# c_gate and h_b of six channel groups computed by tokens, 1024 columns at once, with two seven-product pairs of k-tiles, and a transpose by TensorE

## The chip, the cores and the metric

One core of a Trainium2 chip runs the kernel. The metric is device time of one execution in microseconds (us). Engines: TensorE (PE), VectorE (DVE), ScalarE (ACT), GpSimd (POOL), SyncE (SP, which only issues transfers here).

## The reference

An encoder layer over 256 tokens of 2048 channels, in float32. What touches the change is the second branch, a gated short convolution along the tokens:

```
proj = rmsnorm(h, norm_w) @ w_in          # 9 x 2048 columns
q, v, f_fwd, f_bwd, z_a, b_gate, c_gate, h_b, z_b = split(proj)
o_a = head_rmsnorm(hgrn2(silu(q), v, f_fwd, f_bwd)) * silu(z_a)
y_b = b_gate * short_conv(c_gate * h_b, conv_w)     # width 3, centred, per channel
o_b = rmsnorm(y_b, conv_norm_w) * silu(z_b)
h = h + concat([o_a, o_b]) @ w_out
```

A gate with a second input and a last norm follow.

## The kernel before

**Precision.** A float32 product is made of three products of a rounded high part (`hi`) and the rest (`lo`): hi x hi, hi x lo, lo x hi. The input x, scaled by `norm_w`, is kept split as `xs` (16 k-tiles of 128 channels, hi and lo, 256 tokens). The norm factor per token, `rx`, is multiplied in afterwards.

**Weights.** `Stream` (lines 28 to 134) brings the weights in the order of use. SP loads a `raw` tile of 1 MB (three buffers, and the early ones of the output stage a fourth); each is split into parts of 1024 columns, `spl` (five buffers): ACT casts the high part (line 121), DVE subtracts it for the low part (line 122). `get` asks for three parts ahead of the one in use, at high priority.

**Two ways to multiply.** `gemm_in` (432) gives channels on partitions: a weight k-tile stands still, `xs` streams past, 512 columns (hi and lo of x) and then 256, 32 such pairs for one product of 256 channels. It takes two of the four PSUM banks of the pool `psg`; `evac` (482) empties each with an ACT copy into `r` and a DVE add. `gemm_vz` (456) with `half` (551) gives tokens on partitions: x stands still and 512 weight columns stream. It computes two blocks of 512 columns together, so it takes all four `psg` banks (two token halves by two blocks). Of the eight pairs of k-tiles (q = 0 to 7), those listed in `VZ_SUMS` are multiplied with seven products of 2x2 blocks in place of eight (sums of x made in advance by `act_sums` and `act_split`; sums of weights made in the `raw` tile by three DVE adds, `add_up`, line 79; four more banks for extra products). Such a pair has four `spl` parts instead of two.

**The stage that changes** (924 to 984) is a loop over eight groups of 256 channels. Each group makes four products with `gemm_in`, c_gate (CG), h_b (HB), b_gate (BG), z_b (ZB), then: POOL normalises CG and multiplies by HB into `ub` (channels by tokens, with a zero column at either end); DVE does the convolution into `cg`; POOL multiplies by BG; the square is summed into `ysum`; POOL normalises ZB (`by_norms`), ACT takes its sigmoid `szb`, DVE and POOL multiply all into `cg`; ACT and DVE split `cg` into `mixb` hi and lo. In groups 1 to 4 sums of `mixa` are made too (`sa`, `sb`, `suma`), and in groups 2 to 4 sums of `mixb`, both for the output product.

**Transfers beside.** In this stage the sums of w_out for the later output product are prepared in DRAM: `prepare` copies two blocks into `sums` (SP queue, line 330), `add_up` (332) adds on POOL's queue in three steps. `pump`, called after POOL's operations, does one step at a time, six a group; 16 such sums, 48 steps.

**Order.** A scheduler places the instructions of each engine by priority in the program; each engine runs its own in that fixed order.

## Time and profile before

| | |
|---|---|
| median of 3 runs | 1113.97 us (1111.71 to 1114.72) |
| the profiled execution | 1112.2 us, of which 1110.5 are its span |
| mean granted clock of PE | 0.998 |
| transfers over the span | 260.44 MB, mean 235 GB/s |
| groups 2 to 7 of the stage | some 568 to 835 us |

A row of the timeline has start, length, engine, line, operation, output and inputs, and in brackets the idle time before it and what ended it. SPq is an issue of a transfer by SP. PE's matmuls overlap, so their pitch is read from their starts, not their lengths. In the views of transfers a queue has packets, MB and its share of 16 engines' time.

### The profile page before, as it was taken

What the parts mean: (1) busy time and instruction counts of PE and PEld (TensorE: products, weight loads), DVE (VectorE), ACT (ScalarE), POOL (GpSimd) and SP (SyncE); (2) the same over time, 40 slices, a digit from 0 to 9 for tenths busy, and PEclk for the clock granted to TensorE, in tenths of its full rate; (3) what the DMA queues carried; (4) which work ended last, traced back from release to release, by engine and by line L of the source; (5) the groups of instructions that cost most, each with busy time, mean ns of one, the idle gap of its engine ahead of it and who ended that gap; (6) DMA issues with size and microseconds to landing.
All of it is one profiled execution on the core that took longest, in us unless ns stands there. A gap on an engine that the chain in (4) does not pass through costs nothing.

```text
span 1110.5 us, 16882 instructions
## 1 busy us (share of the span) xinstructions
PE 1100.5 (99%) x6455; PEld 945.7 (85%) x6455; DVE 851.4 (77%) x1127; ACT 677.3 (61%) x946; POOL 269.1 (24%) x215
## 2 busy tenths in 40 slices
PE   9999999999999999999999999999999999999997
PEld 8888888888888888888888888888888888888886
DVE  7799578896889778997657758856667888887673
ACT  6786577667876697575545535535546575575562
POOL 1045015203530325043334223424331000000101
PEclk9999999999999999999999999999999999999999
DMA  9755454564457744758999998999979887887542
GB/s 340 272 187 190 153 190 157 171 242 153 161 162 258 292 152 152 231 172 228 298 310 250 270 334 231 282 345 254 288 196 306 318 299 286 286 312 253 193 133 76
DMA packets 69808, 260.44 MB, mean 235 GB/s; under 512 B 7008, under 2 KB 16608, under 8 KB 52192
## 3 DMA queue, kind: packets, MB, share of 16 engines
q1 hardware_dynamic: 60480, 242.25, 62.1%
q0 software_dynamic: 8960, 16.78, 10.0%
q8 instruction: 51, 0.84, 0.3%
q10 hardware_dynamic: 288, 0.34, 0.1%
q14 instruction: 29, 0.24, 0.1%
HBM read 257.25 MB, written 35.65 MB: 264 GB/s over the span
## 4 chain that ended last, share of the span: by engine, by line
PE 98%; DMA 1%; ACT 0%; SPq 0%; DVE 0%; DVEq 0%; issue 0%; ACTq 0%
PE a L427 37%; PE a L425 19%; PE avz L547 3%; PE avz L548 3%; PE avz L549 3%; PE pg L1027 3%; PE pg L1026 3%; PE pg L1028 3%; PE pa L547 2%; PE pa L548 2%; PE pa L549 2%; PE a L446 1%; PE a L448 1%; PE a L447 1%; PE pb_sc L548 1%; PE pb_sc L549 1%
## 5 line engine op out<-in xcount | busy, mean ns | idle before, releaser
L122 DVE TENSOR_TENSOR spl<-raw,spl 128x1024 fp32r<-128x1024 f32 (+2 forms) x419 | 505.0, 1219 | 163.6 <-ACT spl L121 160.2
L427 PE MATMUL a<-xs,spl 128*128 128x512 f32 x1792 | 617.3, 395 | 0.6 <-ACT spl L121 0.6
L121 ACT CAST spl<-raw 128x1024 fp32r<-128x1024 f32 (+2 forms) x419 | 414.1, 999 | 255.0 <-PE a L425 81.9
L425 PE MATMUL a<-xs,spl 128*128 128x256 f32 x1792 | 483.8, 278 | 0.0
L427 PEld LDWEIGHTS a<-xs,spl 128*128 128x128 f32 x1792 | 332.2, 188 | 73.6 <-ACT spl L121 1.0
L425 PEld LDWEIGHTS a<-xs,spl 128*128 128x128 f32 x1792 | 334.6, 188 | 5.8 <-DVE spl L122 0.5
L1143 POOL TENSOR_TENSOR hh<-hh,fw 128x512 f32<-128x512 f32 (+1 forms) x9 | 11.0, 1227 | 250.7 <-ACT gt L1142 248.0
L487 ACT COPY r<-a 128x256 f32<-128x256 f32 x112 | 40.5, 368 | 37.3 <-PE a L425 35.8
L547 PE MATMUL avz<-spl,xs 128*128 128x512 f32 x138 | 54.0, 391 | 0.0
L549 PE MATMUL avz<-spl,xs 128*128 128x512 f32 x138 | 53.7, 389 | 0.0
L548 PE MATMUL avz<-spl,xs 128*128 128x512 f32 x138 | 53.7, 389 | 0.0
L1026 PE MATMUL pg<-spl,ht 128*128 128x512 f32 (+1 forms) x120 | 45.2, 377 | 0.0
L1027 PE MATMUL pg<-spl,ht 128*128 128x512 f32 (+1 forms) x120 | 45.1, 376 | 0.0
L1028 PE MATMUL pg<-spl,ht 128*128 128x512 f32 (+1 forms) x120 | 45.0, 375 | 0.0
L716 POOL TENSOR_TENSOR qc<-pf,ge 128x256 f32<-128x256 f32 x16 | 18.3, 1148 | 105.8 <-ACT dd L706 91.8
L492 POOL TENSOR_TENSOR xf<-xf,rbc 128x1024 f32<-128x1024 f32 x8 | 19.9, 2486 | 94.0 <-DVE rbc L403 50.2
L121 ACT CAST spl<-early 128x1024 fp32r<-128x1024 f32 (+1 forms) x29 | 28.7, 990 | 19.1 <-PE pb_y L549 7.5
L122 DVE TENSOR_TENSOR spl<-early,spl 128x1024 fp32r<-128x1024 f32 (+1 forms) x29 | 32.9, 1147 | 9.2 <-ACT spl L121 8.8
L547 PE MATMUL pa<-spl,mixa 128*128 128x512 f32 x88 | 34.5, 392 | 0.0
L549 PE MATMUL pa<-spl,mixa 128*128 128x512 f32 x88 | 34.3, 389 | 0.0
L548 PE MATMUL pa<-spl,mixa 128*128 128x512 f32 x88 | 34.2, 389 | 0.0
L716 POOL TENSOR_TENSOR kc<-dd,ge 128x256 f32<-128x256 f32 x16 | 27.7, 1728 | 19.8 <-DVE dd L707 13.6
(321 smaller groups left out, 1641.7 us busy)
## 6 DMA issues: line engine op xcount, KB each, us to landing
raw<-in_w_in_dram SPq DMA_DIRECT2D x106, 1024.0 KB, 6.9
raw<-in_w_in_dram SPq DMA_DIRECT2D x100, 256.0 KB, 3.9
raw<-in_w_out_dram SPq DMA_DIRECT2D x36, 512.0 KB, 5.2
sums<-in_w_out_dram SPq DMA_DIRECT2D x32, 512.0 KB, 10.6
raw<-in_w_in_dram SPq DMA_DIRECT2D x26, 512.0 KB, 5.2
raw<-sums SPq DMA_DIRECT2D x13, 1024.0 KB, 5.3
raw<-in_w_gate_dram SPq DMA_DIRECT2D x9, 1024.0 KB, 5.1
sums<-in_w_out_dram POOLq DMA_DIRECT2D x16, 512.0 KB, 10.1
```

The source lines that it names most:

```text
L121: self.nc.scalar.copy(out=v[:, :, 0], in_=r)
L122: self.nc.vector.tensor_tensor(out=v[:, :, 1], in0=r, in1=v[:, :, 0], op=ALU.subtract)
L425: pe.matmul(a[:, :T], lhsT=lhsT, rhs=xs[:, kt, 0, :], start=False, stop=(kt == NKT - 1))
L427: pe.matmul(a, lhsT=lhsT, rhs=xs[:, kt, :, :].rearrange("p s n -> p (s n)"), start=(kt == 0), stop=False)
L487: act.copy(out=r, in_=acc[m][:, 1, :])
L547: pe.matmul(acc, lhsT=ah, rhs=w[:, 0], start=start, stop=False)
L548: pe.matmul(acc, lhsT=ah, rhs=w[:, 1], start=False, stop=False)
L549: pe.matmul(acc, lhsT=al, rhs=w[:, 0], start=False, stop=stop)
L716: pool.tensor_tensor(out=c64(dst[:, d]), in0=c64(src[:, d, :, half * P : (half + 1) * P]), in1=g.unsqueeze(3).broadcast_to([P, 2, 2, CH]), ...
L1026: pe.matmul(acc[m], lhsT=lh, rhs=wh, start=(kt == 0), stop=False)
L1027: pe.matmul(acc[m], lhsT=lh, rhs=wl, start=False, stop=False)
L1028: pe.matmul(acc[m], lhsT=ll, rhs=wh, start=False, stop=(kt == nk - 1))
```

## The change

For groups 2 to 7, c_gate and h_b of two groups (512 channels each) are one product by tokens, `gemm_pair`, the general form of `gemm_vz`, with pairs q = 2 and 4 as seven products. Three such products (groups 2, 4, 6) replace twelve `gemm_in`. DVE combines the extra products, adds the main ones, and multiplies c_gate, h_b and `rx2` (the square of `rx`); PE turns the result to channels by tokens in eight transposes per product, 12 k-tiles into the next BG, and ACT copies it to `ub`. The convolution then follows. The weights of these products come in four transfers of 256 KB (rows of 2 KB) for each `raw` tile; 1 MB in one transfer (rows of 8 KB) before. The x sums for q = 2 and 4 are kept in the last quarter of `mixa`, the scaled output of the last two heads waits in SBUF and not PSUM, and `mixb` is eight tiles. In groups 2 to 7 `pump` is called four times a group and four times in each of the new products.

```diff
+    CH_SUMS = (2, 4)
+    for i in range(2):
         for c in (B_CG, B_HB, B_BG, B_ZB):
             blocks[c, i] = sum((ws.add(w_in[c + i, h]) for h in range(2)), [])
+    for i in range(2, 8, 2):
+        blocks[B_CG, i] = []
+        for q in VZ_ORDER:
+            srcs = [
+                [w_in[c + i + b, q // 4, :, 2 * (q % 4) : 2 * (q % 4) + 2] for b in range(2)] for c in (B_CG, B_HB)
+            ]
+            blocks[B_CG, i].append(ws.add_own(*srcs) if q in CH_SUMS else ws.add(*srcs[0], *srcs[1]))
+        for ii in (i, i + 1):
+            for c in (B_BG, B_ZB):
+                blocks[c, ii] = sum((ws.add(w_in[c + ii, h]) for h in range(2)), [])
...
+        dve.tensor_tensor(out=rx2, in0=rx, in1=rx, op=ALU.mult)
...
-    def gemm_vz(i, vt, zt):
+    def gemm_pair(name, sums_of, ids, get):
-        acc = [psg.tile([P, 512], F32, tag="g", name=f"avz{i}_{b}") for b in range(4)]
+        acc = [psg.tile([P, 512], F32, tag="g", name=f"a{name}_{b}") for b in range(4)]
...
-        for q1, q5, q6, q7 in half(main, extra, VZ_ORDER, VZ_SUMS, blocks[B_V, i], xs, xq[0], True):
+        for q1, q5, q6, q7 in half(main, extra, VZ_ORDER, sums_of, ids, xs, xq, True):
+            vt, zt, d = get()
...
+    def convolved(i, ut):
+        for ii in (i, i + 1):
+            tp = psm.tile([P, 2, T], F32, tag="xy"[ii % 2], name=f"ut{ii}")
+            for h in range(2):
+                c = (2 * (ii % 2) + h) * P
+                for m in range(2):
+                    pe.transpose(tp[:, h, m * P : (m + 1) * P], ut[:, m, c : c + P], ident)
+            act.copy(out=ub[ii % 2][:, :, 1 : T + 1], in_=tp)
+    def gemm_ch(i):
+        def get():
+            a, b = (bp.tile([P, 2, 512], F32, tag=f"late{e}", name=f"ch{i}_{e}") for e in range(2))
+            return a, b, early[:, 0:512]
+        for z in range(4):
+            at(5 + 10 * z, pump)
+        a, b = gemm_pair(f"ch{i}", CH_SUMS, blocks[B_CG, i], get)
+        with tc.high_priority(offset=300):
+            for m in range(2):
+                dve.scalar_tensor_tensor(
+                    out=a[:, m], in0=a[:, m], scalar=rx2[:, m : m + 1], in1=b[:, m], op0=ALU.mult, op1=ALU.mult
+                )
+        at(12, lambda: convolved(i, a))
     for i in range(8):
-        cg = ctmp.tile([P, 2, T], F32, tag="cg", name=f"cg{i}", bufs=2)
-        evac(gemm_in(B_CG, i, TURNED if i % 2 == 0 else {}), lambda m: cg[:, m, :], ctmp)
-        hb = ctmp.tile([P, 2, T], F32, tag="hb", name=f"hb{i}", bufs=2)
-        evac(gemm_in(B_HB, i, {} if i else TURNED), lambda m: hb[:, m, :], ctmp)
         u = ub[i % 2]
-        by_norms(cg, rbc2, 2)
-        pump()
-        pool.tensor_tensor(out=u[:, :, 1 : T + 1], in0=cg, in1=hb, op=ALU.mult)
-        pump()
+        if i < 2:
...
+        elif i % 2 == 0:
+            gemm_ch(i)
+        kick = {} if i % 2 else TURNED
+        hb = ctmp.tile([P, 2, T], F32, tag="hb", name=f"bg{i}", bufs=2)
+        evac(gemm_in(B_BG, i, kick), lambda m: hb[:, m, :], ctmp)
```

How the order moves is shown at three places. The first is PE's queue in the changed kernel where ZB of group 1 (`a_1_1`, its second bank) ends and the first new product (`ach_0` to `ach_3`, one bank each) begins; `spl_5436` and `spl_5455` are the two parts of its first weight tile.

```order
L437 MATMUL a_1_1_5411<-xs,spl_5412 128x256
L566 MATMUL ach_0_5529<-spl_5436,xs 128x512 [waits DVE_49,Activation_49]
...
L566 MATMUL ach_1_5530<-spl_5436,xs 128x512 [waits DVE_49,PE_49]
...
L566 MATMUL ach_2_5531<-spl_5436,xs 128x512 [waits DVE_49]
...
L566 MATMUL ach_3_5532<-spl_5436,xs 128x512 [waits DVE_49,PE_49]
```

Between the first `ach_0` and the first `ach_3` stand 15 matmuls; each bank's first matmul now waits for the DVE operation that empties it, and the last two banks are those of ZB.

The second is ACT's queue at the same place, first before and then after: `r` is the copy that empties a bank of ZB of group 1, `raw_5537` and `raw_5542` are the third weight tile of what follows.

```order
L487 COPY r<-a_1_0_5402 128x256 [waits DVE_49,PE_49]
L121 CAST spl_5539<-raw_5537 128x4x256 [waits DMAHW2_49,PE_49]
L487 COPY r<-a_1_1_5403 128x256 [waits DVE_49]
L121 CAST spl_5558<-raw_5537 128x4x256 [waits PE_49]
L953 ACTIVATE szb_5494<-hb_5205 128x512 [waits Pool_49]
```

```order
L505 COPY r<-a_1_0_5410 128x256 [waits DVE_49,PE_49]
L121 CAST spl_5547<-raw_5542 128x2x512 [waits DMAHW1_49,DMAHW0_49,PE_49]
L505 COPY r<-a_1_1_5411 128x256 [waits DVE_49]
L1011 ACTIVATE szb_5508<-zb_5409 128x512 [waits Pool_49]
L121 CAST spl_5569<-raw_5542 128x512 [waits DMAHW3_49,DMAHW2_49,PE_49]
L1033 CAST mixb_5115<-cg_5122 128x2x256 [waits Pool_49]
```

The cast of the third tile's first part keeps its place between the two copies, and waits for two of the tile's four transfers now, for its one transfer before.

The third is DVE's queue from there in the changed kernel: the split of that part, the three adds of `add_up` (L83) between the tail of ZB (`zb`, `mixb`) and the sums of `mixa` (`sa`, `sb`, `suma`), up to the split of the fourth tile, `raw_5614`.

```order
L506 TENSOR_TENSOR zb_5409<-a_1_1_5411,r 128x256
L83 TENSOR_TENSOR raw_5542<-raw_5542 128x2x512
L1014 SCALAR_TENSOR_TENSOR zb_5409<-zb_5409,vec,szb_5508 128x256 x2
L122 TENSOR_TENSOR spl_5569<-raw_5542,spl_5569 128x512
L551 TENSOR_TENSOR sa_5518<-mixa 128x512
...
L1034 TENSOR_TENSOR mixb_5115<-cg_5122,mixb_5115 128x2x256
...
L122 TENSOR_TENSOR spl_5584<-raw_5542,spl_5584 128x2x512
...
L122 TENSOR_TENSOR spl_5605<-raw_5542,spl_5605 128x2x512
...
L562 TENSOR_TENSOR suma<-sb_5519,suma 128x3x128
L122 TENSOR_TENSOR spl_5619<-raw_5614,spl_5619 128x1024
```

Before, the third tile needed two splits at this place and no adds; now it needs four splits and three adds, in the same stretch as the tail of group 1.

More of the change, by code (lines that the diff above doesn't have):

```diff
@@ L234, in tile_hymba_encoder @@
     few = const.tile([P, 16], F32, name="few")
-    rx, rb, rf, most, dummy = (few[:, 2 * j : 2 * j + 2] for j in range(5))
+    rx, rb, rf, most, dummy, rx2 = (few[:, 2 * j : 2 * j + 2] for j in range(6))
     xf32 = xp.tile([P, NKT, T], F32, name="xf32")
@@ L477, in gemm_vz @@
                     dve.tensor_tensor(out=dst[:, m], in0=main[m][n], in1=dst[:, m], op=ALU.add)
+        return vt, zt
+    def gemm_vz(i, vt, zt):
+        gemm_pair(f"vz{i}", VZ_SUMS, blocks[B_V, i], lambda: (vt, zt, xd[0][:, 0]))
+        with tc.high_priority(offset=400):
             for dst in (vt, zt):
@@ L517, in tile_hymba_encoder @@
     mixa = mixp.tile([P, NH * 2 * T + 8], F32R, name="mixa")[:, : NH * 2 * T]
+    late = mixa[:, (NH - 4) * 2 * T :].rearrange("p (z o s t) -> p z o s t", z=2, o=4, s=2)
     mixa = mixa.rearrange("p (k s t) -> p k s t", k=NH, s=2)
@@ L567, in half @@
                     for m in range(2):
-                        ah, al = (src[:, k + kk, s, m * P : (m + 1) * P] for s in range(2))
+                        ah, al = (tile_of(src, k + kk)[:, s, m * P : (m + 1) * P] for s in range(2))
                         three(main[m][n], al, ah, w[:, n], q == order[0] and kk == 0, q == order[-1] and kk == 1)
@@ L579, in one @@
             def one(kk, m):
-                return [src[:, k + kk, s, m * P : (m + 1) * P] for s in (1, 0)]
+                return [tile_of(src, k + kk)[:, s, m * P : (m + 1) * P] for s in (1, 0)]
             def some(o):
-                return [src[:, k, s, P:] if o == sums.shape[2] else sums[:, z, o, s] for s in (1, 0)]
+                return [tile_of(src, k)[:, s, P:] if o == sums[z].shape[1] else sums[z][:, o, s] for s in (1, 0)]
             w = ws.get(ids[0])
@@ L899, in keep @@
                 def keep():
-                    kept.extend(psm.tile([P, 2, 2, P], F32, tag=f"sc{e}", name=f"kept{e}") for e in range(2))
+                    kept.extend(t.rearrange("p (m h) t -> p m h t", m=2) for t in scm)
                     finish_two(ogs, ss, zt, kept)
@@ L913, in tile_hymba_encoder @@
     sumb32 = [*scm, tri]
-    mixb = None
     bctx = ExitStack()
@@ L948, in tile_hymba_encoder @@
         pump()
-        evac(gemm_in(B_ZB, i, TURNED if i in (0, 6) else {}), lambda m: hb[:, m, :], ctmp)
+        hb = ctmp.tile([P, 2, T], F32, tag="hb", name=f"zb{i}", bufs=2)
+        evac(gemm_in(B_ZB, i, kick), lambda m: hb[:, m, :], ctmp)
         by_norms(hb, rbc, 2)
@@ L965, in tile_hymba_encoder @@
             bp = mctx.enter_context(tc.tile_pool(name="bp", bufs=1, side="right", reuse_waits="tile"))
-            mixb = bp.tile([P, NH, 2, T], F32R, name="mixb")
             og = bp.tile([P, 2, 2, 2, P], F32, name="og")
             suma = bp.tile([P, len(SUMS), 3, 2, P], F32R, name="suma")
+            mixb.extend(bp.tile([P, 2, 2, T], F32R, name=f"mixb{i}") for i in range(6))
+        if i == 6:
+            mixb.extend(bp.tile([P, 2, 2, T], F32R, tag=f"late{e}", name=f"mixb{i + e}") for e in range(2))
         if i == 2:
@@ L1015, in tile_hymba_encoder @@
     tmp = spare.tile([P, 2, 512], F32, name="tmp")
+    sums_a, sums_b = ([t[:, z] for z in range(len(SUMS))] for t in (suma, sumb))
     tmps = [*(tmp[:, b] for b in range(2)), *(og[:, e].rearrange("p m h t -> p (m h t)") for e in range(2))]
@@ L1072, in tile_hymba_encoder @@
             )
-        for src, sums, main, other, scale in ((mixa, suma, psg, psm, False), (mixb, sumb, psm, psg, True)):
+        for src, sums, main, other, scale in ((mixa, sums_a, psg, psm, False), (mixb, sums_b, psm, psg, True)):
             name = f"p{'ab'[scale]}{u}"
```

36 lines of the change are left out of this document (23 added, 13 removed).

## Prediction

> **What bounds the kernel now.** I read the busy shares first, then the chain of waits that ended last, then whatever TensorE (PE) ever waited for.
>
> ```profile
> PE 1100.5 (99%) x6455; PEld 945.7 (85%) x6455; DVE 851.4 (77%) x1127; ACT 677.3 (61%) x946; POOL 269.1 (24%) x215
> PE 98%; DMA 1%; ACT 0%; SPq 0%; DVE 0%; DVEq 0%; issue 0%; ACTq 0%
> PE wps L266 <- DVE wz L261: 1.1, 1, 1.1
> PE a L427 <- ACT spl L121: 0.6, 1, 0.6
> 568.00:657.00 89.00, 89.00 (x515) 77.83 (x514) 59.62 (x86) 42.58 (x59) 31.66 (x24) 1.00 0.95 282
> ```
>
> PE is busy 99% of the span, 98% of the chain is PE, and all its waits come to 1.7 us. The last row is one pair of channel groups (i=2, 3) in the stage that changes: PE 89.00 of 89.00 us at full granted clock, DVE 59.62, the DMA engines 0.95 busy. So time is PE's columns times its pitch; anything that makes PE wait is added in full.
>
> **What PE saves.** PE's pitch is read from starts in its timeline:
>
> ```profile
> 559.82 0.39 PE L427 MATMUL a<-xs,spl 128*128 128x512 f32 x1
> ...
> 569.18 0.40 PE L427 MATMUL a<-xs,spl 128*128 128x512 f32 x1
> 569.41 0.40 PE L425 MATMUL a<-xs,spl 128*128 128x256 f32 x2
> ...
> 449.63 0.39 PE L549 MATMUL avz<-spl,xs 128*128 128x512 f32 x1
> ...
> 459.83 0.39 PE L549 MATMUL avz<-spl,xs 128*128 128x512 f32 x1
> ...
> 835.00 0.87 PE ogt L658 x8
> ```
>
> From 559.82 to 569.18 stand 27 pairs (512 and 256 columns): 0.3467 us a pair. From 449.63 to 459.83 stand 45 matmuls of 512: 0.2267 us each. Eight transposes take 0.87 us, 0.109 each. Removed: c_gate and h_b of six groups, 12 products of 32 pairs, 384 x 0.3467 = 133.1 us. Added: three products, each six plain pairs of k-tiles (24 matmuls) and two with seven products (21), 186 x 3 = 558 x 0.2267 = 126.5 us; and 24 transposes, 2.6 us. **Net -4.0 us.** The Trainium skill, "TensorE: Matmul & The Clock Gate", Part 4, puts a transpose in a kernel at about 275 ns; by that the 24 would be 6.6 us and the net 0.0. It speaks of a transpose mode; the row above disagrees for these, so the sum goes by the row.
>
> **What makes PE wait: the start of each new product.** It takes four PSUM banks and there are four. Two were left by BG, long free; the other two by the ZB product that has just ended. Matmul 16 (first of `ach_3`) needs ZB's second bank, 15 x 0.2267 = 3.4 us after the start. That bank is emptied by ACT's copy `r` and a DVE add, and in ACT's queue the cast of the third weight tile's first part stands ahead of that copy (shown with the change). Before, the same three rows stand there in the same order:
>
> ```profile
> 568.34 0.37 ACT L487 COPY r<-a 128x256 f32<-128x256 f32 x1 [1.38 <-PE a L425]
> 573.52 1.05 ACT L121 CAST spl<-raw 128x1024 fp32r<-128x1024 f32 x1 [4.81 <-DMA raw<-in_w_in_dram]
> 574.48 0.36 ACT L487 COPY r<-a 128x256 f32<-128x256 f32 x1
> ...
> 662.46 1.05 ACT L121 CAST spl<-raw 128x1024 fp32r<-128x1024 f32 x1 [4.98 <-DMA raw<-in_w_in_dram]
> ...
> 751.43 1.05 ACT L121 CAST spl<-raw 128x1024 fp32r<-128x1024 f32 x1 [5.17 <-DMA raw<-in_w_in_dram]
> ...
> 658.58 0.47 PE a L427 x2
> ...
> 747.35 0.47 PE a L427 x2
> ...
> 540.95 3.64 SPq L330 DMA_DIRECT2D sums<-in_w_out_dram x4
> ...
> 553.18 2.72 SPq L330 DMA_DIRECT2D sums<-in_w_out_dram x4
> 557.15 74.12 SPq L100 DMA_DIRECT2D raw<-in_w_in_dram x14
> ```
>
> The turned order (two 256s at 569.41) marks k-tile 1 of group 2's first product, so that began one k-tile (0.69) before 569.18, at 568.49; likewise, from the doubled 512 at 658.58 and 747.35 less 1.15, groups 4 and 6 began at 657.43 and 746.20. The third tile lands 5.03, 5.03 and 5.23 us after these starts, each time: SP issues eight copies of w_out into `sums` ahead of it (540.95, 553.18), and it follows at 557.15, 16 us before it lands. Today that costs nothing, since the next product takes the two older banks. The change leaves the copies where they are.
>
> Two things shift the landing. The first part now needs half the tile. And the tiles come in 2 KB rows, not 8 KB:
>
> ```profile
> q1 hardware_dynamic: 4205, 24.45, 67.4%
> ...
> q1 hardware_dynamic: 7340, 17.14, 51.3%
> ```
>
> 560 to 660 us (8 KB weight rows) gives 16 x 100 x 0.674 / 24.45 = 44.1 engine-us a MB; 400 to 500 (mostly 2 KB and 1 KB) 47.9, 9% more. A tile of 1.05 MB takes 46/16 = 2.9 us alone, 4.3 with the copies' software queue between; three tiles at 9% more are 1.1 later, half a tile is 2.2 earlier: first part at 5.0 + 1.1 - 2.2 = 3.9. Then cast, split, add:
>
> ```profile
> 614.17 1.23 DVE L122 TENSOR_TENSOR spl<-raw,spl 128x1024 fp32r<-128x1024 f32 x1 [0.53 <-ACT spl L121]
> 615.31 0.42 DVE L488 TENSOR_TENSOR hb<-a,r 128x256 f32<-128x256 f32 x1
> ...
> 618.17 0.87 DVE L956 SCALAR_TENSOR_TENSOR hb<-hb,vec,szb 128x256 f32<-128x256 f32 x2
> 619.08 0.69 DVE L532 TENSOR_TENSOR sa<-mixa 128x512 f32<-128x512 f32 x1
> ...
> 622.13 0.68 DVE L974 TENSOR_TENSOR mixb<-cg,mixb 128x512 fp32r<-128x512 f32 x1
> ...
> 448.64 2.67 DVE L83 TENSOR_TENSOR raw<-raw 128x1024 f32<-128x1024 f32 x3
> 451.22 2.50 DVE L122 TENSOR_TENSOR spl<-raw,spl 128x1024 fp32r<-128x1024 f32 x2
> 454.58 4.34 DVE L122 TENSOR_TENSOR spl<-raw,spl 128x1024 fp32r<-128x1024 f32 x4 [0.86 <-ACT spl L121]
> ...
> 458.01 0.39 PE L547 MATMUL avz<-spl,xs 128*128 128x512 f32 x1
> ...
> 617.20 0.63 ACT L953 ACTIVATE szb<-hb 128x512 f32<-128x512 f32 x1 [0.28 <-POOL hb L492]
> ...
> 620.96 0.62 ACT L973 CAST mixb<-cg 128x512 fp32r<-128x512 f32 x1 [1.27 <-POOL cg L960]
> ...
> L960 POOL TENSOR_TENSOR cg<-cg,hb 128x512 f32<-128x512 f32 x6 | 10.5, 1752 | 6.7 <-DVE hb L956 6.7
> L492 POOL TENSOR_TENSOR hb<-hb,rbc 128x512 f32<-128x512 f32 x6 | 10.3, 1714 | 43.5 <-DVE hb L488 43.5
> ```
>
> Cast 1.05 + split 1.23 + add 0.42 make the bank free at 6.6 against 3.4: **a wait of 3.2 us, three times, 9.6.** Bounds each: nothing (first half there by 0.7), 5.5 (whole tile needed, 6.1 us after the start). I take the middle, since the landing is measured three times within 0.2 us.
>
> **What makes PE wait: the first pair with seven products.** DVE's queue from the freed bank on (call it 0) interleaves the tail of ZB with the work on the third tile: normalising on POOL 1.71, sigmoid 0.63, product 0.87 (3.21); split 0.65, `sa` 0.69, add-up 0.72 (5.27); meanwhile POOL's product 1.75 and ACT's cast 0.62 end at 5.58; `lo` 0.68, add-up 0.72 (6.98); cast 1.05, split 1.23 (9.26); two small sums 0.6, split 1.23, two more 0.6 (11.69); ACT's `suma` cast about 0.5 (from its 384 columns beside 0.62 for 512), then the next tile's cast 1.05 and split 1.23: 14.5. PE, freed at 0, is 3.4 us into its product; its two plain pairs and the first seven products take 48 + 21 matmuls, 15.6, and the split is wanted one matmul later, 15.87: 12.5 from 0. Late by 2.0. The second such pair: from that split DVE needs 0.28 + 1.23 + 1.23 + 0.65 + 2.67 + (cast) 1.05 + 1.23 = 8.3, PE 33 matmuls = 7.5: 0.9 more. In group 4 DVE also makes sums of mixb there (0.69 and small ones): about 0.3 more. In group 6 both kinds of sums are gone (1.8 us of DVE and the `suma` cast), and the margin is about 0.8 us. **So 2.9 + 3.2 = 6 us**; bounds nothing and 9 (all three as group 4). What speaks against it: in the earlier use of this routine (rows at 448 to 458 us) the split of the tile after such a pair ends at 455.8 and PE wants it at 458.0, 2.2 us later; but there nothing else stands between.
>
> **What is hidden.** DVE over a pair of groups: 3 more splits' worth (3.7), add-ups 2 x 2.67, 10 combining operations at about 0.68, less 8 evacuations x 0.42: +12 us on 59.62, 72 of some 87: averaged out, cover enough. ACT and POOL lose work. Transposes come at k-tile 12 of BG, 8.3 us in; DVE has their input by about 3.4. `rx2`, the sums kept in SBUF: nothing on PE's path. PSUM banks for BG are free before its start, since the last pair is done one column half after the other.
>
> **Sum.** -4.0 + 9.6 + 6.0 = +11.6 on the profiled execution's 1112.2 us (its span 1110.5 and 1.7 around it): 1123.8. The median of the runs, 1113.97, is 1.8 above that execution; I keep 1124.
>
> **Rivals.** (a) *PE never waits*, the other side: the first half of the third tile lands within 0.7 us of the start and DVE keeps its 2.2 us lead; then only the PE sum is left, 1108 us. It turns at that landing. Against it: 5.03, 5.03, 5.23. For it: only two of the tile's four transfers are waited for. Chance 0.12. (b) *Only one of the two waits is real*: banks alone 1117.8; splits alone, or shorter bank waits of about 1 us, 1113 to 1116. 0.30, half of it within 0.3% of now. (c) *The waits slow PE's clock.* At the program's start:
>
> ```profile
> 1.13 5.74 PE L266 MATMUL wps<-wz 128*128 128x128 f32 x26 [1.13 <-DVE wz L261]
> ```
>
> 26 matmuls of 128 columns take 0.22 us each against 0.109 later: half speed for 5.7 us after idling. If each bank wait did that, 2.9 us each: 1132. The same page of the skill (Part 1) says that an idle window of 3413 ns brings the clock to half. No row here shows an idle PE in mid-run. Chance 0.10. (d) *DMA becomes the bound*: 25 MB of weights at 3.8 engine-us a MB more is 6 us of 266, 0.95 to 0.97; it would show as late tiles in BG and ZB too, some 1130. 0.05. (e) PE's count is not what I read: 0.02. The forecast: 0.41.
>
> **Numbers.** The chance of slower by over 0.3% (3.3 us, about what a measurement of this kernel can tell from no change): the forecast, (c), (d) and half of (b), 0.71; within: 0.16; faster: 0.13. The range runs from 1110, near (a) measured against the median, to 1133, which takes in (c) and the upper bound of the bank wait.
>
> **What would show it.** In the profile after: PE waits on DVE at the first `ach` matmuls of bank four, about 3 us, three times; PE waits on splits at the tile after the second pair in groups 2 and 4; ACT's cast of the third tile waiting for DMA ahead of its second `r`; 0.227 us pitch elsewhere. No PE wait at these places proves me wrong; so does a landing before 0.7 us.

## The result, and the profile after

| | before | after |
|---|---|---|
| median | 1112.84 us (4 runs, 1111.67 to 1114.72) | 1153.78 us (4 runs, 1149.17 to 1155.81) |
| the profiled execution, its span | 1112.2, 1110.5 us | 1155.8, 1154.1 us |

The ratio is 1.036, 95% interval 1.0325 to 1.0396: slower, as forecast, but by 41 us where 10 were forecast, and far beyond the range.

The page of after, busy shares and the chain of waits:

```profile
PE 1111.8 (96%) x6269; PEld 944.9 (82%) x6269; DVE 890.8 (77%) x1164; ACT 684.4 (59%) x943; POOL 247.1 (21%) x203
PE 81%; DMA 11%; DVE 5%; ACT 1%; SPq 1%; POOL 0%; issue 0%; DVEq 0%; ACTq 0%; POOLq 0%
```

PE has 186 matmuls fewer, and yet it is busy 11 us longer: a first sign that some of them ran slowly. The chain has fallen from 98% PE to 81%, and DMA is what came in. What PE waited for, in the new products:

```profile
PE ach L566 <- DVE zb L506: 22.3, 5, 6.9
PE ach L566 <- ACT spl L121: 6.0, 3, 2.7
PE ach L567 <- DVE spl L122: 4.2, 5, 1.3
```

`zb` is the emptying of ZB's banks, `spl` a split of weights. The stage by stretches, each new product and, for one pair of groups, the BG and ZB products behind it (columns: length and PE busy, then the other engines, PE's granted clock, the DMA share):

```profile
567.04:622.20 55.16, 46.55 (x189) 37.35 (x188) 35.81 (x45) 22.21 (x27) 9.58 (x8) 0.91 0.89 236
622.20:667.52 45.32, 45.32 (x266) 39.73 (x264) 33.35 (x50) 19.93 (x27) 9.52 (x9) 1.00 0.78 230
667.52:727.63 60.11, 47.61 (x189) 37.41 (x187) 42.74 (x56) 25.13 (x32) 13.24 (x12) 0.86 0.89 247
772.96:832.59 59.63, 48.24 (x188) 37.81 (x187) 41.22 (x45) 24.50 (x29) 12.90 (x12) 0.86 0.93 253
```

BG and ZB run without a wait at full clock. The three products take 55.16, 60.11 and 59.63 us for 186 x 0.2267 = 42.17 us of work, at granted clocks of 0.91, 0.86 and 0.86. All of the loss is there. In the first of them, PE:

```profile
570.22 0.39 PE L568 MATMUL ach<-spl,xs 128*128 128x512 f32 x1
575.75 0.77 PE L566 MATMUL ach<-spl,xs 128*128 128x512 f32 x1 [5.14 <-DVE zb L506]
576.32 0.63 PE L567 MATMUL ach<-spl,xs 128*128 128x512 f32 x1
576.74 0.63 PE L568 MATMUL ach<-spl,xs 128*128 128x512 f32 x1
...
600.20 0.39 PE L568 MATMUL scps<-spl,mixa 128*128 128x512 f32 x1
603.30 0.49 PE L566 MATMUL ach<-spl,xs 128*128 128x512 f32 x1 [2.71 <-ACT spl L121]
604.56 0.80 PE L567 MATMUL ach<-spl,xs 128*128 128x512 f32 x1 [0.77 <-DVE spl L122]
605.15 0.63 PE L568 MATMUL ach<-spl,xs 128*128 128x512 f32 x1
```

The sixteenth matmul waits for ZB's second bank, as forecast, but 5.3 us (from start to start, less one pitch). Behind it the pitch is 0.43 us in place of 0.23: half clock. A second wait, forecast by nobody, comes at 600 us: the first part of the tile of q = 5, behind the second pair with seven products. Sorted in this way from PE's starts (gaps over 0.6 us; what is left over 42.17 us is put down to the half clock):

| product | length | idle at its start | idle at q = 5 | lost at half clock |
|---|---|---|---|---|
| group 2 | 55.16 | 5.3 | 3.9 | 3.8 |
| group 4 | 60.11 | 10.8 | 2.9 | 4.3 |
| group 6 | 59.63 | 9.8 | 2.8 | 4.9 |
| sum | 174.9 | 25.9 | 9.6 | 12.9 |

48.4 us in all. With PE's forecast saving of 4.0, and 1.45 us by which the stage already starts earlier (567.04 against 568.49), 43.0 of the 43.6 us between the two spans are accounted for. The 1.45 us are no effect of the change: e10 below, up to there the kernel before, has the two 256s that mark this start at 567.59 in place of 569.41, and so begins at 566.67. The doubled pitches of group 2, added up by themselves, lose 3.5 us, near the 3.8 of the table.

Not all of the idle time at the starts is at the sixteenth matmul. In groups 4 and 6 PE also waits for the split of the first tile (0.8 and 1.5 us) and for ZB's first bank (2.6 in both), 7.5 of the 25.9 us; the prediction has a wait at neither.

Behind the waits stand late tiles. ACT of after:

```profile
566.89 0.37 ACT L505 COPY r<-a 128x256 f32<-128x256 f32 x1 [1.38 <-PE a L437]
572.97 1.04 ACT L121 CAST spl<-raw 128x1024 fp32r<-128x1024 f32 x1 [5.70 <-DMA raw<-in_w_in_dram]
573.92 0.37 ACT L505 COPY r<-a 128x256 f32<-128x256 f32 x1
...
602.20 1.04 ACT L121 CAST spl<-raw 128x1024 fp32r<-128x1024 f32 x1 [6.17 <-DMA raw<-in_w_in_dram]
```

The rows of step A: the cast of the third tile ahead of the second `r`, 5.9 us after the start where 3.9 was forecast. SP's issues of after (x4 are the parts of one tile, or the copies of two sums):

```profile
554.56 3.83 SPq L341 DMA_DIRECT2D sums<-in_w_out_dram  x4
558.56 2.29 SPq L96 DMA_DIRECT2D raw<-in_w_in_dram  x4
...
586.27 6.05 SPq L100 DMA_DIRECT2D raw<-in_w_in_dram  x8
...
661.50 3.10 SPq L341 DMA_DIRECT2D sums<-in_w_out_dram  x4
664.81 3.15 SPq L96 DMA_DIRECT2D raw<-in_w_in_dram  x4
```

The third tile is issued 8.5 us ahead of group 2's product, behind four copies of w_out, and its first part needs 14.4 us until the cast; in group 4 it is issued 2.7 us ahead, again behind copies, and in group 6 1.8. In before it was 11.3 us ahead (557.15 to 568.49). The tile of q = 5, the first four of the eight issues at 586.27, needs 16 us to land. What ran beside it shows on POOL, in before first:

```profile
588.22 4.48 POOL L492 TENSOR_TENSOR cg<-cg,early 128x512 f32<-128x512 f32 x1 [5.54 <-DVE cg L488]
592.65 1.03 POOL L338 DMA_DIRECT2D sums<-in_w_out_dram  x1
595.33 1.29 POOL L932 TENSOR_TENSOR ub<-cg,hb 128x512 f32<-128x512 f32 x1 [1.65 <-DVE hb L488]
596.57 1.07 POOL L338 DMA_DIRECT2D sums<-in_w_out_dram  x1
604.79 1.29 POOL L943 TENSOR_TENSOR cg<-cg,hb 128x512 f32<-128x512 f32 x1 [7.14 <-DVE hb L488]
606.02 1.06 POOL L338 DMA_DIRECT2D sums<-in_w_out_dram  x1
606.83 1.59 POOL L947 TENSOR_TENSOR ysum<-ysum,y 128x512 f32<-128x512 f32 x1
608.27 1.16 POOL L338 DMA_DIRECT2D sums<-in_w_out_dram  x1
```

and in after:

```profile
579.61 1.61 POOL L1018 TENSOR_TENSOR cg<-cg,zb 128x512 f32<-128x512 f32 x1 [0.97 <-DVE zb L1014]
581.16 0.82 POOL L353 DMA_DIRECT2D sums<-sums  x1
581.71 4.54 POOL L349 DMA_DIRECT2D sums<-in_w_out_dram  x4
```

In before each accumulating copy of 512 KB stands behind a POOL product, and three of the four products wait for work that follows the group's matmuls, so four copies spread over 16 us. The change takes two of these products (normalising CG, times HB) off POOL. Its four calls of `pump` are spaced in the program (at counts 5, 15, 25 and 35, a count being three matmuls here, so 6.8 us of PE's work apart), but on POOL there is nothing between them, and they go out in 4.5 us. The queues of after from 586 to 606 us:

```profile
q0 software_dynamic: 1056, 2.03, 63.1%
q1 hardware_dynamic: 1630, 2.98, 41.6%
```

POOL's queue moves 2.03 MB and takes 16 x 20 x 0.631 / 2.03 = 99 engine-us a MB (time of one of the 16 DMA engines); SP's queue with the tiles 45. So four accumulating copies at once weigh as much as more than four tiles. The price is not new: in the same 20 us of before POOL's queue took 108 engine-us a MB, but moved 1.08 MB, and the tiles got 4.32 MB through in place of 2.98.

### The profile page after: what moved, and what is told of

It is laid out like the page before. It is cut to its first block, busy times and chain, and to the rows that moved or that the text cites. A ratio compares the mean times of both kernels' runs of the same rounds, so it can differ in the third digit from the quotient of the medians.

```text
span 1154.1 us, 16646 instructions
## 1 busy us (share of the span) xinstructions
PE 1111.8 (96%) x6269; PEld 944.9 (82%) x6269; DVE 890.8 (77%) x1164; ACT 684.4 (59%) x943; POOL 247.1 (21%) x203
## 2 busy tenths in 40 slices
DMA packets 83248, 260.43 MB, mean 226 GB/s; under 512 B 8160, under 2 KB 23904, under 8 KB 68704
## 4 chain that ended last, share of the span: by engine, by line
PE 81%; DMA 11%; DVE 5%; ACT 1%; SPq 1%; POOL 0%; issue 0%; DVEq 0%; ACTq 0%; POOLq 0%
PE a L439 23%; PE a L437 11%; DMA raw<-in_w_in_dram 9%; PE avz L568 3%; PE avz L566 3%; PE avz L567 3%; PE pg L1088 3%; PE pg L1089 3%; DVE spl L122 3%; PE pg L1087 3%; DMA sums<-in_w_out_dram 2%; PE ach L567 2%; PE ach L568 2%; PE pa L566 2%; PE pa L568 2%; PE pa L567 2%
## 5 line engine op out<-in xcount | busy, mean ns | idle before, releaser
L122 DVE TENSOR_TENSOR spl<-raw,spl 128x1024 fp32r<-128x1024 f32 (+2 forms) x431 | 515.4, 1210 | 180.2 <-ACT spl L121 164.1
L121 ACT CAST spl<-raw 128x1024 fp32r<-128x1024 f32 (+2 forms) x431 | 423.5, 994 | 305.1 <-PE a L437 69.3
L439 PE MATMUL a<-xs,spl 128*128 128x512 f32 x1408 | 483.8, 395 | 0.0
L437 PE MATMUL a<-xs,spl 128*128 128x256 f32 x1408 | 376.5, 278 | 0.0
L439 PEld LDWEIGHTS a<-xs,spl 128*128 128x128 f32 x1408 | 260.0, 188 | 55.3
L437 PEld LDWEIGHTS a<-xs,spl 128*128 128x128 f32 x1408 | 262.5, 188 | 5.6
L566 PE MATMUL ach<-spl,xs 128*128 128x512 f32 x156 | 66.7, 427 | 28.3 <-DVE zb L506 22.3
L567 PE MATMUL ach<-spl,xs 128*128 128x512 f32 x156 | 66.1, 424 | 4.2 <-DVE spl L122 4.2
L568 PE MATMUL ach<-spl,xs 128*128 128x512 f32 x156 | 65.3, 418 | 0.0
L566 PEld LDWEIGHTS ach<-spl,xs 128*128 128x128 f32 x156 | 32.2, 207 | 39.1 <-issue 19.1
L1000 POOL TENSOR_TENSOR cg<-cg,bg 128x512 f32<-128x512 f32 x8 | 11.8, 1469 | 206.4 <-DVE bg L506 206.4
L505 ACT COPY r<-a 128x256 f32<-128x256 f32 x88 | 31.6, 368 | 27.0 <-PE a L437 26.9
L83 DVE TENSOR_TENSOR raw<-raw 128x512 f32<-128x512 f32 (+1 forms) x45 | 42.2, 938 | 1.0 <-DMA raw<-in_w_in_dram 0.2
L567 PEld LDWEIGHTS ach<-spl,xs 128*128 128x128 f32 x156 | 32.3, 207 | 12.6 <-DVE spl L122 6.0
```

The source lines that it names most:

```text
L83: self.nc.vector.tensor_tensor(out=out, in0=out, in1=other, op=ALU.add)
L121: self.nc.scalar.copy(out=v[:, :, 0], in_=r)
L122: self.nc.vector.tensor_tensor(out=v[:, :, 1], in0=r, in1=v[:, :, 0], op=ALU.subtract)
L437: pe.matmul(a[:, :T], lhsT=lhsT, rhs=xs[:, kt, 0, :], start=False, stop=(kt == NKT - 1))
L439: pe.matmul(a, lhsT=lhsT, rhs=xs[:, kt, :, :].rearrange("p s n -> p (s n)"), start=(kt == 0), stop=False)
L505: act.copy(out=r, in_=acc[m][:, 1, :])
```

## The experiments

Most runs ask for the cause; the last group looks for a place of the w_out traffic that leaves the saving. Times without an interval are of one execution, beside medians of 1111.7 to 1112.7 of the kernel before on the same chips.

| run | time, us | products 2, 4, 6, us | longest PE waits elsewhere, us |
|---|---|---|---|
| after | 1153.8 | 55.2, 60.1, 59.6 | none |
| e1_early | 1159.0 | 55.7, 60.2, 61.2 | 0.4 |
| e2_phase | 1125.0 | 46.6, 45.4, 45.4 | 3.5 and 0.8, group 1 |
| e3_both | 1130.0 | 46.2, 49.6, 44.9 | 3.7 and 0.5, group 1 |
| e4b_plain | 1154.3 | 52.5, 59.0, 60.6 | 0.5 |
| e5_own | 1127.2 | 42.9, 43.0, 42.2 | output projection (other work there) |
| e6_fill | 1160.6 | 57.3, 61.4, 60.1 | 0.3 |
| e9_whole | 1136.4 | 48.0, 54.2, 53.6 | none |
| e10_fine (of before) | 1114.2 | | 0.9 and 0.6 |
| e11_noacc | 1165.6 | 50.6, 59.0, 58.6 | 4.2 and 5.0 ahead of the last two, 4.1 behind the stage (for POOL's `ysum`) |
| e14_rows_order | 1129.3 | 45.7, 50.5, 50.8 | 0.8 |
| e7_spread | 1115.6 | 43.0, 43.7, 43.1 | 1.6 and 0.8, heads' last product |
| e8_heads | 1118.9 | 43.0, 43.6, 42.2 | 5.5, heads' last product |
| e8b_group0 | 1124.3 | 43.2, 43.9, 42.2 | 9.3, heads (behind POOL) |
| e15_later, e18_last | 1123.4, 1123.0 | 42.9, 46.5, 43.4; 42.9, 44.5, 43.0 | 6.2, 7.1, output projection |
| e16_later_whole, e17_last_whole | 1120.3, 1120.9 | 42.9, 43.0, 42.2 in both | 5.2, 5.6, output projection |
| e19_before_heads | 1108.6 | 42.9, 43.1, 42.2 | 0.2 |

### Order of the queue, or place of the copies

```diff
-        evac(gemm_in(B_ZB, i, kick), lambda m: hb[:, m, :], ctmp)
+        evac(gemm_in(B_ZB, i, kick), lambda m: hb[:, m, :], ctmp, 500 if i in (1, 3, 5) else 200)
```

> One edit to the changed kernel: ACT's copies and DVE's adds that empty ZB's two banks ahead of each new product get a priority that puts them in front of the cast of the third weight tile. Theory 'order' (the bank is late only because its copy stands behind a cast that waits for DMA): the 25.9 us of PE idle time at the starts of the three new products (5.3, 10.8, 9.8) go, and with them the half-clock stretches that follow (about 2.2, 2.5 and 3.1 us of them lost), 1154 - 34 = about 1120. Theory 'late tiles' (the weights themselves land too late for PE, the bank only hides it): PE then waits for the split of the second or third tile instead, 2 to 8 us per product in groups 4 and 6, and the time is 1135 to 1150. Both: the later wait, about 3 us at the sixth pair of k-tiles (q = 5), stays.

Measured 1159.0: neither number. The waits of e1_early:

```profile
PE ach L566 <- ACT spl L121: 9.8, 4, 3.9
PE ach L567 <- DVE spl L122: 7.4, 9, 1.6
PE ach L566 <- DVE zb L506: 4.9, 2, 2.5
PE eych L567 <- DVE spl L122: 2.7, 3, 1.0
```

The bank's 22.3 us fell to 4.9, but the waits for splits rose from 10.2 to 22.5; the products are as long as before the edit. The bank was where the shortage showed, not where it came from: 'late tiles', and stronger than I had put it.

```diff
             by_norms(cg, rbc2, 2)
             pump()
             pool.tensor_tensor(out=u[:, :, 1 : T + 1], in0=cg, in1=hb, op=ALU.mult)
             pump()
+            pump()
+            pump()
```

(for groups 0 and 1 only, so that all later steps fall a third of a round earlier)

> One edit to the changed kernel: two more steps of the w_out preparation in each of groups 0 and 1, so that every copy of w_out into sums is issued about half a pair of groups earlier and none stands in SP's queue just ahead of a new product's tiles. Theory 'copies' (the third tile is late because eight copies of 512 KB stand ahead of it): ACT's cast of that tile waits under 2 us for DMA in place of 5.7, PE's idle time at the three starts falls from 25.9 to under 8 us, and the time to 1120 to 1130. Theory 'held buffers' (SP can't issue the tile sooner, since only three buffers hold tiles): the landing moves by less than 2 us and the time stays at 1145 to 1156. The wait at q = 5 should also shrink if the accumulating copies on POOL's queue, which ran beside that tile's load, were its cause: from 3.9 to under 1 us in group 2.

Measured 1125.0: 'copies'. No stretch at half clock is left in the products, and 4.3 us of waits have come in group 1, where the copies now are. The third tile is issued 7.7 us ahead of group 2's product, no sooner than in after, but with no copies just ahead of it, and is cast 8.0 us later in place of 14.4 (566.13 to 574.12): in group 2 what it shares the engines with makes it late, more than the moment of its issue. At q = 5 in group 2 1.4 + 1.0 us stay idle: less, but not under 1. (The accumulating copies of 512 KB now stand behind POOL products of group 1, from 571.36 to 583.33 us.)

> The two edits together: banks emptied in front of the cast, and the w_out copies half a pair of groups earlier. If the waits at the starts have two causes that each hold them alone, this is faster than either alone; if 'order' is enough it is within 3 us of the first of the two, about 1120. If the wait at q = 5 is due to held buffers, 9.6 us of idle time and about 5 us at half clock remain, so not below 1115; if it was the accumulating copies, 1106.

Both edits together, 1130.0: the copies' place decides, and emptying the banks first, which holds up splits, came out 5 us dearer with either place (single executions).

### The tiles: held buffers, rows, the sum of all traffic

```diff
-    CH_SUMS = (2, 4)
+    CH_SUMS = ()
...
```

(without such pairs there are no sums to add to; ACT copies the four banks out instead)

> One edit to the changed kernel, whose w_out copies stay where they are: no pair of k-tiles as seven products in the new products, all eight pairs as eight (their four banks are then copied out in place of the sums). PE's own work grows by 6 x 3 x 0.2267 = 4.1 us. Theory 'held buffers' (the tile of such a pair keeps its buffer until its sums are split, so the tile three later, q = 5, is issued late): the wait at q = 5 goes in all three products (9.6 us idle, about 5 lost at half clock): 1154 + 4 - 15 = 1143. Theory 'accumulating copies' (the load of q = 5 shares the DMA engines with POOL's accumulating copies, which the pairs do not change): that wait stays, about 3 us each, and the time is 1155 to 1160. The waits at the starts stay under both.

Measured 1154.3, between the two. The wait at q = 5 went, as 'held buffers' said, but the wait for ZB's banks grew from 22.3 to 29.1 us: PE lost at the start what it no longer lost later.

```diff
-                    sums = dramp.tile([P, 4, 512], F32, name=f"sums{u}_{half}_{q}")
-                    prepared.append((srcs, sums))
-                    oblocks[-1].append(ws.add_sums(*srcs, sums))
+                    oblocks[-1].append(ws.add_own(*srcs))
...
```

(and the first four copies, beside the last pair of heads, are left out)

> The changed kernel without any preparation of w_out in this stage: no copies into sums on SP, no accumulating copies on POOL; the output projection makes its sums from its own tiles, as the new products do. Read in the stage of the new products alone (the output stage gets other work, so the total says less): theory 'w_out traffic' (all waits come from transfers that share SP's queue and the DMA engines): the three products take 42.2 to 43.5 us each in place of 55.2, 60.1 and 59.6, with no half-clock stretch. Theory 'held buffers': the starts recover, but a wait of 2 to 4 us at q = 5 stays in each. Theory 'DVE queue' (my step B): waits on splits at the first pair with seven products or right behind it, 1 to 3 us in groups 2 and 4, none in 6.

The products of e5_own, and ACT and PE in the first:

```profile
567.19:610.12 42.93, 42.46 (x188) 34.85 (x187) 35.68 (x44) 21.99 (x27) 3.82 (x2) 1.00 0.58 196
655.44:698.48 43.04, 42.47 (x188) 34.86 (x187) 36.74 (x50) 22.16 (x28) 3.82 (x2) 1.00 0.57 199
743.81:786.00 42.19, 42.19 (x188) 34.94 (x187) 33.54 (x37) 21.66 (x25) 3.81 (x2) 1.00 0.60 203
```

```profile
567.05 0.37 ACT L503 COPY r<-a 128x256 f32<-128x256 f32 x1 [1.39 <-PE a L435]
567.39 1.05 ACT L121 CAST spl<-raw 128x1024 fp32r<-128x1024 f32 x1
568.34 0.37 ACT L503 COPY r<-a 128x256 f32<-128x256 f32 x1
```

```profile
583.70 0.50 PE L565 MATMUL ach<-spl,xs 128*128 128x512 f32 x1 [0.47 <-DVE spl L122]
```

'w_out traffic', wholly: 128.2 us for 126.5 of work. The cast stands ahead of the second `r` as ever, but its tile is there, so nobody waits. What remains is one short wait each in groups 2 and 4 (0.6 and 0.7 us) and none in group 6, at the tile behind the first pair with seven products: my step B, in its place, at about a fifth of its size.

```diff
-            blocks[B_CG, i].append(ws.add_own(*srcs) if q in CH_SUMS else ws.add(*srcs[0], *srcs[1]))
+            ws.whole[len(ws.todo)] = w_ch[i // 2 - 1, q]
+            blocks[B_CG, i].append(ws.add_own(*srcs) if q in CH_SUMS else ws.add(*srcs[0], *srcs[1]))
```

(`w_ch` holds the same weights, laid out by tiles; `load` brings a tile of `whole` in one transfer)

> One edit to the changed kernel: the tiles of the new products lie in DRAM as they are wanted in SBUF, so each comes as one transfer of 1 MB with rows of 8 KB, in place of four of 256 KB with rows of 2 KB; everything else, the w_out preparation too, stays. Theory 'rows' (small rows and many transfers make the supply late): the third tile lands 2 to 3 us sooner, and the three products shorten from 55, 60, 60 us to 44 to 50: 1115 to 1130. Theory 'w_out traffic' (what the tiles share the engines and SP's queue with): tiles take 9% less engine time, 0.3 us each, some 2 us a product, while the first part now waits for the whole tile: 1146 to 1156.

Measured 1136.4, between the two: rows and transfers matter more than 9% of a tile's time, as long as the traffic stands beside them. All that is left of the waits:

```profile
PE ach L572 <- DVE zb L512: 22.0, 5, 7.0
```

So the wait at q = 5 went here too. It went in each run that took one of three things out: the buffer held by the second pair (e4b), the accumulating copies beside it (e11), the small rows (e9). That it needs all three at once is a reading of these three runs; each also changed when PE came to q = 5.

```diff
+            if j in self.fine:
+                for q in range(4):
+                    self.nc.sync.dma_start(dst[:, b, 2 * q : 2 * q + 2], src[:, 2 * q : 2 * q + 2])
```

(in the kernel before, for c_gate and h_b of groups 2 to 7)

> The kernel before, with one edit: the tiles of c_gate and h_b in groups 2 to 7 come as four transfers of 256 KB with rows of 2 KB in place of one of 1 MB with rows of 8 KB. If small rows are what starves the new products, PE waits for splits here too, 3 us or more at each group pair: 1122 or more. If they cost only 9% of DMA time in part of the stage and the lead of the tiles covers it: 1111 to 1116, the third tile of c_gate landing some 1 us later than 5.0 after the start.

Measured 1114.2, one wait of 0.9 us in the stage: small rows alone starve nothing, where tiles come as early as in before.

```diff
-        for z in range(4):
-            at(5 + 10 * z, pump)
         a, b = gemm_pair(f"ch{i}", CH_SUMS, blocks[B_CG, i], get)
```

(and two more calls of `pump` in each of groups 2 to 7, behind the square)

> The changed kernel with no step of the w_out preparation during a new product: the four that stood there go to the two groups behind it, two more in each, and the order of steps is the same, so the copies into sums still stand just ahead of the next product. Theory 'copies ahead' (they alone start the shortage): the starts keep their waits, products 52 to 60 us, and only the wait at q = 5 goes: 1140 to 1150. Theory 'accumulating copies beside' (POOL's transfers, at 87 engine-us a MB against 44 to 50 for tiles, take the engines from the product's own tiles): products fall to 44 to 48 us: 1112 to 1125.

Measured 1165.6, more than both: the wait at q = 5 went, but the steps that were pushed together ahead of the next product, with the copies, made the second and third product wait 4.2 and 5.0 us before their first matmul. Taking the steps out of the product gains nothing when they bunch up just ahead of the next one.

> The changed kernel with two edits together: tiles of the new products as one transfer of 1 MB with 8 KB rows, and the copies and adds that empty ZB's banks in front of the cast of the third tile. The w_out preparation stays where it is. Theory 'order and rows' (with the supply 9% quicker, the bank is all that holds PE, 22.0 us of waits and the half clock behind them): both go, the products take 42 to 45 us: 1109 to 1116. Theory 'shortage' (copies ahead of the product leave too little time for its tiles): the waits move from the bank to splits of the second and third tile, as they did with the order alone: 1125 to 1137.

The edits of e1 and e9 together, 1129.3: 'shortage', by the time and in part by the waits. The wait for ZB's second bank is gone, but 2.6, 5.3 and 4.3 us a product are idle still (gaps over 0.6 us): 7.5 of the 12.2 us for splits, the other 4.7 for ZB's first bank in groups 4 and 6.

### The clock

```diff
...
+                        if fill is not None and q == order[0] and n == 1 and kk == 0 and m == 1:
+                            for _ in range(24):
+                                pe.matmul(fill, lhsT=ah, rhs=w[:, n, 0], start=True, stop=True)
```

> The changed kernel with 24 extra matmuls of 512 columns (5.4 us at the usual pitch) into a bank that is used later, ahead of the matmul that waited for ZB's second bank (5.3, 7.3 and 5.7 us); their result is overwritten. Theory 'clock' (the idle time itself halves PE's clock for what follows): the extra matmuls stand where PE idled, so they cost nothing, and the half-clock stretches that began there go (2.2 us lost in group 2, less than all of 2.5 and 3.1 in groups 4 and 6, where another wait of 2.9 us precedes): 1154 - 3 to 7 = 1147 to 1151. Theory 'no link' (the half clock comes from elsewhere, or the waits move with PE's start): the extra matmuls add up to 3 x 5.4 less the idle time, 1154 to 1160, and the stretches stay.

Measured 1160.6: 'the waits move'. The waits for the second bank are gone, and in group 2 no pitch is doubled up to q = 5 where 10 were in after, so the idle time was what slowed the clock. But PE, ready sooner, waits for the next tiles, and slows down there: 16.3 us of extra work took the place of 10.7 us of idle time (35.5 to 24.8), and the three products together are 3.9 us longer. What sets their length is the supply of tiles.

### Another place for the traffic

```diff
+            for z in range(6):
+                at(140 + 4 * z, pump)
...
-        for z in range(4):
-            at(5 + 10 * z, pump)
...
+        if i >= 2:
+            for z in range(6):
+                at(3 + 5 * z, pump)
```

(first lines in the last pair of heads; the last in each group, in place of its four calls)

> The changed kernel with the preparation of w_out placed anew: none of its steps falls into a new product, its first six steps lie at the end of the heads' stage, the copies for the next four in the even group behind a new product, five k-tiles apart, and the first accumulating copies in the odd group. Theory 'w_out traffic': the waits at the starts and at q = 5 go; what is left is the DVE queue, 0 to 3 us a product, so PE's sum of -4 comes through in part: 1107 to 1116. Theory 'held buffers': as above plus 2 to 4 us at q = 5 in each: 1116 to 1124. If the DMA engines as a whole are the bound in this stage (rival d), moving transfers only moves the waits into BG and ZB: 1125 or more, with PE waits on splits there.

Measured 1115.6, in the first range: the products are at 43.0 to 43.7, and the first steps now stand beside the last heads' product, where PE waits for splits.

> As the run that spread the preparation (1115.6), with its six first steps moved from the end of the last heads' product, where PE had waited 3.8 us for splits of that product's tiles, into the projections ahead of it. If those waits came from the steps beside that product, they go and nothing replaces them: 1110 to 1113, a ratio of about 0.998 to 1.000 to the kernel before. If they move into the projections instead: 1114 to 1117.

`at(140 + 4 * z, pump)` became `at(48 + 8 * z, pump)`. 1118.9, ratio 1.006 (1.0043 to 1.0077), above both ranges: PE waits 5.5 us for a bank at the start of the last heads' product, the same kind of wait as in the new ones.

> As the two runs that spread the preparation, but with nothing of it in the heads' stage beyond what was there: twelve steps in group 0, five k-tiles apart, six in group 1, then six in each group of BG and ZB, none in a new product. If the wait of 5.8 us in the heads came from the steps there, it goes; if twelve steps are too many for group 0, PE waits for splits there or in group 1, 2 to 5 us: 1110 to 1117. With no such wait: PE's sum of -4 less about 2.5 us of waits in the products: 1110 to 1112, a ratio of 0.998 to 1.000.

Twelve steps in group 0 and none in the heads: 1124.3, ratio 1.0107 (1.0091 to 1.0122), above the range. Its wait is of another kind:

```profile
PE o L820 <- POOL s L807: 9.3, 2, 5.4
```

POOL issues the steps itself, in its own queue; the masked scores `s` that the heads' last output product wants stood behind them.

```diff
...
+        if i in (2, 4, 6):
+            for z in range(4):
+                at(2 + 6 * z, lambda n=2 * i + z: prepare(prepared[n]))
+        if i > 2:
+            for z in range(6):
+                at(4 + 5 * z, pump)
...
+    for z in range(6):
+        at(6 + 6 * z, pump)
```

(`pump` no longer starts copies itself; its former calls in groups 2 to 7 and in the new products are gone)

> Another place of the w_out preparation: the first twelve steps as in the kernel before, in groups 0 and 1, the copies for the next four in the even group behind a new product, six k-tiles apart, their steps six in the odd group and six in the next even one; the last six fall into the output projection. None stands in a new product or in the group ahead of one, but for accumulating copies. If the traffic is the whole cause, products of 42 to 44 us and no other wait in this stage: 1109 to 1113, unless the output projection waits for splits (it has six accumulating copies beside it): then up to 1116.

> The same place of the w_out preparation and the tiles of the new products as one transfer of 1 MB with rows of 8 KB. If the change's own saving on PE (4 us) exists and only supply hid it, nothing in the new products waits, and the time is 4 us under the kernel before, 1107 to 1110, a ratio of 0.995 to 0.998. If PE's sum was not as I counted, 1111 to 1114.

1123.4, ratio 1.0104 (1.0085 to 1.0123), and with whole tiles 1120.3, 1.0073 (1.006 to 1.0086), both above what was expected. In the second the products are as in e5, and the output projection begins at 831.18 us, 3.7 sooner than before's 834.84 (2.2 of it won in the stage, which began at 566.98); there PE then waits for a late tile:

```profile
PE pa L570 <- ACT spl L125: 5.2, 1, 5.2
```

> As the run with the later preparation and whole tiles (1120.3), with its last six steps 12 or more k-tiles further back in the output projection and four apart. If the wait of 5.5 us there, and the half clock behind it, came from accumulating copies beside that tile, both go: 1120.3 - 6.0 - 2.2 - 5 (half of the 10.2 us at half clock) = 1107 to 1111, a ratio of 0.995 to 0.999, and the saving on PE is real. If they move along with the steps: 1115 to 1120.

> The same placement with the tiles of the new products as the change loads them (four transfers of 256 KB, rows of 2 KB). The run before with these tiles had waits of 3.8 and 1.1 us in groups 4 and 6, where the one with whole tiles had 0.7 and none: so 3 to 4 us more than the run beside it, 1111 to 1115, if the small rows cost only what they cost there.

`at(6 + 6 * z, pump)` became `at(18 + 4 * z, pump)`: 1120.9, ratio 1.0073 (1.006 to 1.0087), and 1123.0, 1.0083 (1.0067 to 1.0098); both above what was expected. The waits stayed, and so did the steps. POOL of e17_last_whole:

```profile
835.72 0.81 POOL L359 DMA_DIRECT2D sums<-sums  x1 [4.25 <-DMA sums<-in_w_out_dram]
839.46 0.81 POOL L359 DMA_DIRECT2D sums<-sums  x1 [2.93 <-DMA sums<-in_w_out_dram]
...
847.67 0.81 POOL L359 DMA_DIRECT2D sums<-sums  x1 [0.93 <-DMA sums<-sums]
```

The last six steps go out from 836 to 848 us, and from 835 to 847 in e16, though the first of them stands 12 counts later in the program (the last one 2): in POOL's queue they wait for transfers alone, and nothing that waits for PE is between them. The product that normalises the last ZB stands behind them, at 848.21. It is the same mechanism as in the new products. Small rows cost 3.0 and 2.1 us in the two pairs of runs, but in both pairs the intervals overlap.

```diff
-        if i == 6:
+        if i == 4:
             for z in range(4):
                 at(10 + 10 * z, lambda z=z: prepare(prepared[z]))
+        if i == 6:
+            for z in range(6):
+                at(4 + 8 * z, pump)
```

(with e7's six calls a group, and whole tiles)

> Whole tiles for the new products, and the w_out preparation placed as in the run that spread it, with its beginning earlier: the first copies beside the third pair of heads, the first six steps beside the first projections of the last pair (at about 374 to 390 us, behind POOL's own work there), then six steps in each group, none in a new product and none in the output projection. The products have the tiles of the run beside the later placement: 42.2 to 43.0 us each. If nothing waits in the heads either, the output projection starts 3 to 3.7 us sooner than in the kernel before and the time follows: 1108 to 1111, a ratio of 0.996 to 0.999. If PE waits in the heads' products again (5.8 us there in the run with steps in those projections, at 433 us), 1114 to 1119.

1108.64 us (5 runs, 1108.6 to 1108.9), ratio 0.996 (0.9946 to 0.9974): 0.4% under the kernel before, and in the expected range. The products, and where the output projection begins:

```profile
567.30:610.24 42.94, 42.47 (x188) 34.84 (x187) 35.56 (x44) 21.98 (x27) 7.83 (x7) 1.00 0.89 270
655.57:698.64 43.07, 42.51 (x189) 34.83 (x187) 36.73 (x50) 22.18 (x28) 6.20 (x5) 1.00 0.89 272
743.97:786.16 42.19, 42.19 (x189) 34.92 (x187) 33.56 (x37) 21.65 (x25) 6.76 (x6) 1.00 0.86 262
```

```profile
831.56 1.04 PE L687 MATMUL ogt<-ident,og 128*128 128x128 f32 x8
```

The whole kernel moves the same MB as after (260.42 and 260.43), and in BG and ZB of groups 2 to 5 the DMA engines are now fully busy (share 1.01, 299 and 301 GB/s) without a wait of PE there. So the sum of the traffic over the stage was not the bound; when the transfers ran was. In the two profiled executions the stage is 2.1 us shorter than in before; the other 1.2 us between the spans lie ahead of it (567.30 against 568.49), and e10 shows that the start differs so much without the change.

## Why the prediction was right in direction and wrong in size

- **PE's sum, -4.0: right.** In e19 the stage takes 831.56 - 567.30 = 264.26 us against 834.84 - 568.49 = 266.35; less the 1.7 us by which its products exceed 126.5, that is -3.8. The transposes take what the row of before said, 0.109 us from start to start (8 in 1.03 us), while each lasts 270 to 273 ns. The Trainium skill, "TensorE: Matmul & The Clock Gate", Part 4, gives about 275 ns for one; the trace agrees with it as a duration. The prediction set this duration against a pitch and called it a disagreement; its sum, by the pitch, was right.
- **The step that failed: the transfers beside the product were taken as they were in before.** It stands in two sentences of the prediction. One is in step A, "The change leaves the copies where they are", the other under "What is hidden", "ACT and POOL lose work". Three terms come of it: the idle time at the starts (9.6 us forecast, 25.9 measured), a wait at q = 5 (none forecast, 9.6 measured), and the half clock behind both (outside the sum, 12.9 measured). With the w_out traffic gone (e5) or moved (e7, e16, e19) the three products together exceed their 126.5 us by 1.7 to 3.3.
- **Step A, the bank: right place, wrong size.** The landing at 3.9 us was worked out from three rows of before that agreed within 0.2 us, as if the transfers stayed as they were while their consumer changed. It came at 5.9 in group 2, and in group 4 the tile was issued 5.8 us later against the start than in group 2. Three equal rows showed only that before repeats itself. (The 9% for small rows was also read from a mixture: from 400 to 500 us ten tiles of 1 MB came beside 32 transfers of 256 KB.)
- **"ACT and POOL lose work".** POOL's lost products had spaced the accumulating copies; without them four go out at once, at 99 engine-us a MB. The wait at q = 5 went when they were taken out of the product (e11), and in group 2 it fell from 3.9 to 2.4 us in e2, where they stood behind POOL products, but also earlier. That the place of the w_out traffic makes the products long or short is shown; the share of the spacing alone, with the copies left in their place, is not.
- **Step B, the split queue: right groups, 6 us forecast, 1.3 measured** once the tiles are there (e5), all of it behind the first pair; the 0.9 us behind the second did not come. In after it is hidden behind the other waits.
- **Rival (c), the clock: given 0.10, and real:** 12.9 us of the account. By the Trainium skill, same page, Part 1, an idle window of 3413 ns halves the clock; the trace agrees that waits of 5.3 us do it. The two idle spells of 2.9 and 1.0 us at q = 5, with one matmul between them, did it too. I had priced it as an alternative to the waits, not as their consequence. e6, which took the first slow stretches away, gained nothing by it, since the tiles were no sooner there.
- **Rival (d), DMA as the bound:** not as put. Waits came in the products alone, none in BG and ZB, and e19 moves the same MB with two waits of 0.7 us or less in the stage.
- **The range** ended at 1133 because each bound took one step at its worst and the others as forecast. Late tiles work on all of them together.

## What to carry to other kernels

Work on an engine can be what spaces the transfers that the same engine issues: when such work is taken away, ask what then goes out at once, and beside whose tiles. The place of an issue in the program sets its time only if something ahead of it in its engine's queue waits for the work that it is to follow. Where a wait is removed and the time stays, the next wait may be the same shortage in another place: here moving the transfers (the preparation of w_out), and not the waiters, together with tiles in one transfer each, turned a loss of 41 us into a gain of 0.4%.

## What the runs showed of the hardware

- Accumulating copies between DRAM buffers on POOL's queue took 99 engine-us a MB beside tiles that took 45 in the same 20 us (after, 586 to 606 us); in the same stretch of before 108.
- After idle spells of 4.1 to 7.3 us in mid-run (e9 and after) PE's pitch for 512 columns was 0.43 us in place of 0.23, for 3 to 5 us after the data had come.
- Rows of 2 KB in four transfers, in place of 8 KB in one, cost 2 to 3 us at most where tiles were early (e10 beside before, e15 beside e16, e18 beside e17; no more than the runs of one kernel spread) and 17 us where they were late (after beside one execution of e9).
